# Four of the twelve modulation vectors: their rows weighed and added on GpSimd, the partitions summed on TensorE

## The chip, the cores and the metric

The kernel runs on one core of a Trainium2 chip. The metric is the device time of one execution in microseconds (us), as the median of several runs. The core has TensorE (PE in the profile, with its weight loads as PEld), VectorE (DVE), ScalarE (ACT), GpSimd (POOL) and SyncE (SP, which here issues nearly all DMA transfers). SBUF and PSUM are the on-chip memories; PSUM has eight banks, numbered 0 to 7, into which TensorE writes.

## What is computed

Two layers of a diffusion backbone work on 384 tokens: 128 of a prompt and 256 of a sample, each with 1024 channels. Each layer first turns a condition vector (one for the prompt, one for the sample) into six modulation vectors of 1024 numbers, and uses them around its mixers and its FFN:

```python
mod = (jax.nn.silu(cond) @ lp["w_mod"] + lp["b_mod"])[:, None, :]
sh1, sc1, g1, sh2, sc2, g2 = jnp.split(mod, MOD_CHUNKS, axis=-1)
h = rms_norm(x, lp["norm1"]) * (1 + sc1) + sh1
o, new_ctx = token_mixers(h, lp, ctx_cache, rope_a, rope_b)
x = x + g1 * o
h = rms_norm(x, lp["norm2"]) * (1 + sc2) + sh2
x = x + g2 * conv_ffn(h, lp)
```

`w_mod` of a layer has 1024 rows and 6144 columns in fp32, 24 MB. `token_mixers` projects `h` once and runs grouped-query attention (GQA, branch A, 8 heads of 64), multi-head latent attention (MLA, branch B) and a Hyena long convolution (branch C); three gates and three branch projections are merged and projected out.

The vectors are numbered v = 0 to 5 in the order of the split. So v = 3 and 4 (`sh2`, `sc2`) are first needed when the FFN of their layer begins, and v = 5 (`g2`) where its result is added to x.

## The kernel before

**Main products.** Every large product is made of blocks of 128 channels by 384 tokens. `mm3` (lines 268 to 271) makes one fp32 product from three matmuls over split parts: high by high, high by low, low by high. `load_w` (line 247) brings a block of weights by a DMA from SP (line 249) into one of two 1 MB slots (`raw_ring`, inside the slab `base`), copies its high part with ScalarE (line 231) and subtracts it with VectorE (line 235) into the slab `split`.

**Modulation.** `mod_vec` (line 332) makes one of the twelve vectors: four DMAs of 1 MB through the same `raw_ring`, 16 fp32 matmuls of 512 columns whose stationary operand has 32 columns, the condition vectors (line 338; they run in four groups of four, and the profile has two records for each fp32 matmul, so a group shows as x8), a ScalarE copy of 128x512 out of PSUM, four transposes (line 302) and two additions on VectorE. It uses the PSUM line `md`, which is bank 7 and nobody else's.

**Order within a layer.** `weave` (line 1334) advances a main generator and, at given rates, side generators. Layer 0 goes: first Hyena projections; the others with the Hyena chain (`hyena_chain`) beside them; the attention projections; then gates 2, branch 2, gates 0, branch 0, gates 1 with the attention (`att`: `prep`, then `gqa`, then `mla`) beside them; branch 1; the output projection; the FFN. Branch 0 needs GQA's result `oA`, branch 1 MLA's `oB`. In layer 0 v = 2 to 5 are one side chain (`md`, rate 0.24) beside all that; v = 4 of layer 1 comes after the vectors that were begun in layer 0's FFN. On top of this a tile scheduler, which simulates the program in time while it is built, fixes each engine's final order; at run time each engine works its list strictly in that order.

**Attention.** `attention` (line 906) makes scores (line 922), a softmax (`softmax`, line 885: row maximum on VectorE, lines 891 and 892, exponentials on ScalarE, line 894, the scaling on VectorE), transposes (line 302), ScalarE copies and the product with the values (line 954). Its PSUM tiles come from the line `at`, which has banks 3 to 6.

**Banks.** `ps_of(line, ...)` takes the next bank of a line's list, and `banks(...)` sets the lists for each stage:

```python
PS_HY0 = {"mm": "123", "tr": "46", "fl": "05"}
PS_HY1 = {"mm": "0123", "tr": "4", "ch": "56"}
PS_AT = {"mm": "012", "at": "3456"}
PS_OUT = {"mm": "0123", "tr": "456"}
```

Two tiles in one bank follow each other in program order: the later one's first write waits until the earlier one has been read.

**GpSimd** holds 133 instructions. Most belong to the Hyena chain: 128x256 additions and products (line 709) and 128x128 copies (line 658). Products of 128x768 (line 566) and attention copies (line 875) are among the rest.

## Time and profile before

| | us |
|---|---|
| three runs | 1506.55, 1504.46, 1502.84 |
| median | 1504.46 |
| the profiled execution | 1503.74 |
| its span in the profile | 1501.6 |

The mean granted TensorE clock of the profiled execution is 0.992 of full speed. Of the span, PE is busy for 97%, VectorE 67%, ScalarE 50% and GpSimd 7%; the 16 DMA engines are busy for about 43%. A "wait" row says which engine, tile and line waited, and for what. A group row gives a line, engine, operation, output and input with their shapes, a count, and then its busy time, the mean length of one in ns and the idle time of the engine before it. Matmuls overlap in the records (one of 384 columns shows 0.34 us, while the next begins 0.17 to 0.18 us later), so their price is read from the starts of successive rows.

### The profile page before, as it was taken

The numbers are of one execution on the slowest core, as the hardware profiler recorded it, in microseconds if no ns is written. First come the engines' busy times: TensorE is split into PE (matmuls) and PEld (weight loads), VectorE is DVE, ScalarE is ACT, GpSimd is POOL, SyncE is SP. The second block draws the span as 40 slices with busy tenths as digits, with TensorE's granted clock in tenths as the row PEclk, the third lists the DMA queues.
The fourth block names the chain that finished last, engine by engine and source line by source line (L and its number), as shares of the span: only waits on it lengthen the run. The fifth ranks groups of instructions, "written<-read, shape, count | busy, mean of one in ns | idle before, by whom it ended". The sixth has DMA issues, their size and how long they took to land.

```text
span 1501.6 us, 22071 instructions
## 1 busy us (share of the span) xinstructions
PE 1455.7 (97%) x8542; PEld 1337.6 (89%) x8542; DVE 1006.0 (67%) x1920; ACT 751.3 (50%) x1376; POOL 106.4 (7%) x133
## 2 busy tenths in 40 slices
PE   5799999999999999999998999999999999999997
PEld 2588789989889899999996988999888989999997
DVE  6768569547457896686766767884655767567674
ACT  4545356555544663463545444855555454344343
POOL 1223210000000001010000212100000000000000
PEclk9899999999999999999999999999999999999999
DMA  9444454433466543343276446332333523433431
GB/s 362 151 153 138 136 166 138 119 113 113 141 224 228 187 137 103 122 130 113 85 246 204 139 135 182 91 106 83 97 118 111 195 100 117 135 105 122 153 119 50
DMA packets 177496, 212.84 MB, mean 142 GB/s; under 512 B 24176, under 2 KB 160112, under 8 KB 177392
## 3 DMA queue, kind: packets, MB, share of 16 engines
q1 hardware_dynamic: 176528, 206.99, 42.7%
q0 software_dynamic: 864, 4.46, 1.0%
q8 instruction: 67, 1.10, 0.3%
q14 instruction: 37, 0.30, 0.1%
HBM read 209.29 MB, written 2.13 MB: 141 GB/s over the span
## 4 chain that ended last, share of the span: by engine, by line
PE 90%; DVE 4%; ACT 3%; DMA 2%; issue 1%; SPq 0%; DVEq 0%; ACTq 0%
PE banks L269 26%; PE banks L270 26%; PE banks L271 25%; PE banks L302 3%; PE banks L338 3%; PE banks L922 3%; DVE s L238 2%; PE banks L954 2%; DMA base<-in_w_in_dram 1%; DVE split L235 1%; PE banks L558 1%; ACT split L231 1%; ACT s L231 1%; PE banks L503 0%; DVE s L241 0%
## 5 line engine op out<-in xcount | busy, mean ns | idle before, releaser
L231 ACT ACTIVATE split<-base 128x1024 fp32r<-128x1024 f32 (+2 forms) x272 | 280.9, 1041 | 366.9 <-PE banks L270 258.5
L235 DVE TENSOR_TENSOR split<-base,split 128x1024 fp32r<-128x1024 f32 (+2 forms) x272 | 331.8, 1225 | 181.5 <-ACT split L231 179.4
L269 PE MATMUL banks<-h,split 128*128 128x384 f32 x1280 | 433.3, 342 | 5.0 <-DVE h L403 3.6
L270 PE MATMUL banks<-h,split 128*128 128x384 f32 x1280 | 435.2, 340 | 0.1
L271 PE MATMUL banks<-h,split 128*128 128x384 f32 x1280 | 434.2, 340 | 0.0
L269 PEld LDWEIGHTS banks<-h,split 128*128 128x128 f32 x1280 | 241.4, 189 | 20.7 <-issue 9.9
L270 PEld LDWEIGHTS banks<-h,split 128*128 128x128 f32 x1280 | 242.0, 189 | 4.5 <-issue 1.3
L271 PEld LDWEIGHTS banks<-h,split 128*128 128x128 f32 x1280 | 241.7, 189 | 2.2 <-issue 0.5
L270 PE MATMUL banks<-s,split 128*128 128x384 f32 x672 | 225.8, 337 | 0.0
L271 PE MATMUL banks<-s,split 128*128 128x384 f32 x672 | 225.4, 338 | 0.0
L269 PE MATMUL banks<-s,split 128*128 128x384 f32 x672 | 223.2, 339 | 1.0 <-ACT s L231 0.8
L241 DVE SCALAR_TENSOR_TENSOR s<-banks,base,s 128x127 f32<-128x127 f32 (+1 forms) x448 | 172.8, 411 | 11.9 <-ACT s L417 7.9
L231 ACT ACTIVATE s<-banks 128x384 f32<-128x384 f32 (+11 forms) x212 | 94.3, 471 | 99.1 <-PE banks L271 37.9
L231 ACT ACTIVATE s<-s 128x384 fp32r<-128x384 f32 (+3 forms) x142 | 79.0, 562 | 106.0 <-DVE s L238 57.2
L269 PEld LDWEIGHTS banks<-s,split 128*128 128x128 f32 x672 | 125.6, 188 | 4.4 <-ACT s L231 1.4
L271 PEld LDWEIGHTS banks<-s,split 128*128 128x128 f32 x672 | 126.1, 188 | 2.0 <-DVE base L241 0.8
L270 PEld LDWEIGHTS banks<-s,split 128*128 128x128 f32 x672 | 126.1, 188 | 1.4 <-issue 0.2
L238 DVE TENSOR_TENSOR s<-banks,s 128x512 f32<-128x512 f32 (+3 forms) x132 | 81.6, 645 | 37.7 <-PE banks L271 16.7
L241 DVE SCALAR_TENSOR_TENSOR base<-banks,base 128x128 f32<-128x128 f32 (+1 forms) x128 | 46.9, 413 | 73.8 <-PE banks L271 73.8
L238 DVE TENSOR_TENSOR s<-s 128x256 f32<-128x256 f32 (+4 forms) x122 | 69.0, 576 | 23.0 <-ACT s L1225 8.4
L417 ACT ACTIVATE s<-banks,base 128x384 f32<-128x384 f32 x112 | 73.2, 655 | 13.2 <-PE banks L271 13.2
L302 PE MATMUL banks<-base,s 128*128 128x128 f32 x442 | 75.2, 274 | 2.8 <-DVE s L241 1.7
(146 smaller groups left out, 1730.4 us busy)
## 6 DMA issues: line engine op xcount, KB each, us to landing
base<-in_w_in_dram SPq DMA_DIRECT2D x40, 1024.0 KB, 5.4
base<-in_ffn_up_dram SPq DMA_DIRECT2D x40, 1024.0 KB, 5.1
base<-in_w_mod_dram SPq DMA_DIRECT2D x28, 1024.0 KB, 5.3
s<-in_w_mod_dram SPq DMA_DIRECT2D x14, 1024.0 KB, 7.5
base<-in_ffn_down_dram SPq DMA_DIRECT2D x16, 896.0 KB, 4.6
base<-in_w_branch_dram SPq DMA_DIRECT2D x24, 512.0 KB, 3.5
base<-in_w_out_dram SPq DMA_DIRECT2D x8, 1024.0 KB, 5.1
base<-in_ffn_down_dram SPq DMA_DIRECT2D x8, 1024.0 KB, 5.0
```

The source lines that it names most:

```text
L231: act.activation(out=out, in_=in_, func=AF.Copy, scale=scale)
L235: dve.tensor_tensor(out=lo, in0=src, in1=f(hi), op=ALU.subtract)
L238: dve.tensor_tensor(out=out, in0=a, in1=b, op=op)
L241: dve.scalar_tensor_tensor(out=out, in0=a, scalar=s, in1=b, op0=op0, op1=op1)
L269: pe.matmul(out, l[0], r[0], start=start, stop=False)
L270: pe.matmul(out, l[0], r[1], start=False, stop=False)
L271: pe.matmul(out, l[1], r[0], start=False, stop=stop)
L302: pe.transpose(out, in_, ident[:n, :n])
L338: pe.matmul(gv[32 * j:32 * j + 32], cT[:, 2 * k + j // 2], raw[:, j // 2, (j % 2) * 512:(j % 2) * 512 + 512], start=k == 0, stop=k == KD / ...
L417: act.activation(out=dst, in_=src, func=AF.Identity, scale=vec(l, w1), bias=vec(l, bias))
L922: pe.matmul(out, q_of(h)[:, i * 128:(i + 1) * 128], k, start=m == 0, stop=m == len(ks) - 1)
L954: last = pe.matmul(p[b:b + 64, u], v, pT, start=start, stop=stop, tile_position=(0, b)).ins
```

## The change

Three vectors of layer 0 (v = 3, 4, 5) and one of layer 1 (v = 4) leave `mod_vec` and are made by the new `mod_pool`. It works on half a vector, 512 columns, at a time. For each of the 8 blocks of 128 rows of `w_mod` a DMA of 256 KB brings 128x512 numbers into a ring of two slots in the slab `extra`; GpSimd multiplies them by the condition of the sample and of the prompt (two `tensor_scalar`, one number per partition) and adds them to two accumulators (two `tensor_tensor`, none for the first block). So the 1024 rows become 128 partial rows on the partitions. At the end `sums_of` lets TensorE sum over the partitions: 8 matmuls whose stationary operand is a 128x128 piece of the accumulator and whose moving operand is one column of ones. Their results go to PSUM line `tr`, and VectorE adds the bias. v = 3 and 4 are woven (rate 0.8) beside the Hyena and attention projections and finished in program order before the attention begins; v = 5 beside branch 1 and the output projection.

```diff
+    def mod_pool(l, vs):
+        ring, accs, pr_b = Ring(XO, 2, 512), Ring(XO, 2, 1024), XO.alloc(512)
+        late = []
+        def sums_of(v, hf, acc):
+            pm = ps_of("tr", 4, 2)
+            for q in range(4):
+                for s in range(2):
+                    pe.matmul(
+                        pm[:, q, s:s + 1], acc[:, s, q * 128:(q + 1) * 128], ones[:, 0:1], start=True, stop=True
+                    )
+            o = v * 8 + 4 * hf
+            out = mods[l][:, o:o + 4]
+            tt(out, pm, vecs[l][:, V_B + o:V_B + o + 4].unsqueeze(2).to_broadcast([128, 4, 2]), ALU.add)
...
+        for v, hf in [(v, hf) for v in vs for hf in range(2)]:
+            acc = accs.get().ap(2, 512)
+            col = v * 1024 + hf * 512
+            for k in range(KD):
+                raw = ring.get().ap()
+                sp.dma_start(out=raw, in_=w_mod[l, k * 128:(k + 1) * 128, col:col + 512])
+                parts = [pr_b.ap(), raw] if k else [acc[:, 1], acc[:, 0]]
+                for s, out in zip((1, 0), parts):
+                    pool.tensor_scalar(out=out, in0=raw, scalar1=cT[:, k, s:s + 1], scalar2=None, op0=ALU.mult)
+                    if k:
+                        pool.tensor_tensor(out=acc[:, s], in0=acc[:, s], in1=out, op=ALU.add)
+                yield
+                if k == 3 and late:
+                    sums_of(*late.pop(0))
+                    yield
+            late.append((v, hf, acc))
...
+        sums_of(*late.pop(0))
...
     for l in range(NL):
-        md = chain(*[mod_vec(l, v) for v in (2, 3, 4, 5)]) if l == 0 else chain(nxt.pop().steps, mod_vec(l, 4))
+        md = mod_vec(l, 2) if l == 0 else nxt.pop().steps
+        mp = mod_pool(l, (3, 4) if l == 0 else (4,))
         banks(**PS_HY0)
-        weave(main, (md, R_MD), (fl, R_FL))
+        weave(main, (md, R_MD), (mp, R_MP), (fl, R_FL))
...
-        weave(attn_proj(l, hT, proj), (md, R_MD), (ch, R_CH))
+        weave(attn_proj(l, hT, proj), (md, R_MD), (mp, R_MP), (ch, R_CH))
+        finish(mp)
         finish(ch)
         hyena_close(y)
         banks(**PS_AT)
...
-        weave(branch(l, 1, gs, oB, m, merged), (md, R_MD))
+        mp = mod_pool(l, (5,)) if l == 0 else iter(())
+        weave(branch(l, 1, gs, oB, m, merged), (md, R_MD), (mp, R_MP))
...
-        weave(out_proj(l, merged), (ah.loads, R_AH))
+        weave(out_proj(l, merged), (ah.loads, R_AH), (mp, R_MP))
+        finish(mp)
```

In counts: 128 records of modulation matmuls, 16 transposes, 4 ScalarE copies of 128x512 and 16 DMAs of 1 MB go; 64 one-column matmuls, 128 GpSimd multiplications and 112 GpSimd additions of 128x512 and 64 DMAs of 256 KB come. GpSimd's list grows from 133 to some 373 instructions. The lines after the new function move: mm3's three matmuls are now 271 to 273, transposes 304, the scores 968, the product with the values 1000, the Hyena chain's operations 704 and 755; the new DMA is line 390, the multiplication 393, the addition 395, the sums 374.

**TensorE, layer 0, beside the GQA.** The order before, with L269 to L271 the main products (here of branch 2), L922 the scores and L302 the transposes:

```order
L338 MATMUL banks<-base_101 32x512 x4
L269 MATMUL banks<-s_2_702,split_362 128x384
L270 MATMUL banks<-s_2_702,split_362 128x384
L271 MATMUL banks<-s_2_702,split_362 128x384
L302 MATMUL banks<-base_101,s_1_141 128x128 x8
L269 MATMUL banks<-s_2_702,split_362 128x384
L270 MATMUL banks<-s_2_702,split_362 128x384
L271 MATMUL banks<-s_2_702,split_362 128x384
L922 MATMUL banks<-s_4_1554,s_1_135 128x384
L922 MATMUL banks<-s_2_734,s_1_135 128x384
```

The main products stood between the steps of the attention. The order after, at the fourth group of sums (L374), with L271 to L273 the last main products of gates 0, L304 the transposes and L968 the scores:

```order
L271 MATMUL banks<-h_363,split_362 128x384
L272 MATMUL banks<-h_363,split_362 128x384
L273 MATMUL banks<-h_363,split_362 128x384
L374 MATMUL banks<-base_101,extra_470 128x1 x8
L304 MATMUL banks<-base_101,s_1_110 128x128 x4
L968 MATMUL banks<-s_4_1725,s_1_135 128x128
L968 MATMUL banks<-s_2_781,s_1_135 128x128
```

All main products up to the end of gates 0 now stand ahead of the sums, and the attention's first scores behind them. Some 30 rows later on TensorE, in the middle of the same GQA:

```order
L304 MATMUL banks<-base_101,s_1_110 128x128 x6
L968 MATMUL banks<-s_4_1725,s_1_135 128x384
L968 MATMUL banks<-s_2_781,s_1_135 128x384
L304 MATMUL banks<-base_101,s_1_138 128x128 x6
L968 MATMUL banks<-s_4_1725,s_1_135 128x384
L968 MATMUL banks<-s_2_781,s_1_135 128x384
L304 MATMUL banks<-base_101,s_1_141 128x128 x12
```

No main product stands between the attention's steps there any more.

**GpSimd, layer 0, the Hyena chain.** Before:

```order
L658 COPY s_1_107<-s_1_107 128x128 x3
L709 TENSOR_TENSOR s_1_141<-s_1_141,s_1_138 128x256 x2
L709 TENSOR_TENSOR s_1_138<-s_1_138,s_1_141 128x256 x2
L658 COPY s_1_107<-s_1_107 128x128 x2
L709 TENSOR_TENSOR s_1_138<-s_1_138 128x256 x2
```

After:

```order
L395 TENSOR_TENSOR extra_470<-extra_470 128x512
L755 TENSOR_TENSOR s_1_141<-s_1_141,s_1_138 128x256 x2
L704 COPY s_1_107<-s_1_107 128x128
L393 TENSOR_SCALAR extra_470<-extra_470,base_101 128x512
L755 TENSOR_TENSOR s_1_138<-s_1_138,s_1_141 128x256 x2
L395 TENSOR_TENSOR extra_470<-extra_470 128x512
L393 TENSOR_SCALAR extra_470<-extra_470,base_101 128x512
L704 COPY s_1_107<-s_1_107 128x128
```

The chain's instructions (now L704 and L755) have the new multiplications and additions between them.

**SP, layer 0, around the attention projections.** Before, with L249 the weights of `load_w` and L329 the 1 MB loads of `mod_vec`:

```order
L329 DMA base_101<-in_w_mod_dram 128x2x1024
L249 DMA base_101<-in_w_in_dram 128x8x256
L1111 DMA base_101<-in_mla_w_ukv_dram 128x4x64 x4
L249 DMA base_101<-in_w_branch_dram 128x4x256 x4
L249 DMA base_101<-in_w_in_dram 128x8x256 x2
L329 DMA base_101<-in_w_mod_dram 128x2x1024
```

After, with the last four loads of layer 0's v = 4 (L390; L251 is `load_w`):

```order
L390 DMA extra_470<-in_w_mod_dram 128x512
L251 DMA base_101<-in_w_branch_dram 128x4x256
L390 DMA extra_470<-in_w_mod_dram 128x512
L251 DMA base_101<-in_w_branch_dram 128x4x256
L390 DMA extra_470<-in_w_mod_dram 128x512
L251 DMA base_101<-in_w_in_dram 128x8x256
L390 DMA extra_470<-in_w_mod_dram 128x512
```

The small loads of the modulation weights stand one by one between the loads of branch and gate weights.

## Rows read from the trace of the kernel before

**Rows 1.** Page: busy time by engine, then the chain that ended last

```profile
PE 1455.7 (97%) x8542; PEld 1337.6 (89%) x8542; DVE 1006.0 (67%) x1920; ACT 751.3 (50%) x1376; POOL 106.4 (7%) x133
...
PE 90%; DVE 4%; ACT 3%; DMA 2%; issue 1%; SPq 0%; DVEq 0%; ACTq 0%
```

**Rows 2.** PE's waits: line, releaser: us in total, times, longest us

```profile
PE banks L464 <- ACT s L436: 8.6, 1, 8.6
...
PE banks L269 <- DVE h L403: 3.6, 2, 2.3
...
PE banks L269 <- ACT split L231: 0.8, 2, 0.5
```

**Rows 3.** Windows: us, busy of PE, PEld, DVE, ACT, POOL, PEclk, DMA share, GB/s

```profile
245.90:341.30 95.40, 93.75 (x599) 85.52 (x599) 54.88 (x103) 53.41 (x120) 0.45 (x3) 1.00 0.44 125
130.00:216.00 86.00, 86.00 (x476) 71.91 (x475) 55.96 (x95) 37.34 (x68) 21.28 (x22) 1.00 0.48 157
480.00:520.00 40.00, 39.40 (x241) 30.98 (x240) 31.57 (x72) 25.28 (x43) 1.27 (x2) 1.00 0.60 196
520.00:580.00 60.00, 60.00 (x353) 59.26 (x353) 49.72 (x100) 34.33 (x56) 2.56 (x3) 1.00 0.32 106
```

**Rows 4.** Timeline of PE: start us, length, around one group of mod_vec

```profile
237.58 0.34 PE L271 MATMUL banks<-h,split 128*128 128x384 f32 x1
237.85 1.06 PE L338 MATMUL banks<-base 128*32 128x512 f32 x8
...
239.13 0.34 PE L270 MATMUL banks<-h,split 128*128 128x384 f32 x1
```

**Rows 5.** The same, around four transposes

```profile
235.16 0.34 PE L270 MATMUL banks<-h,split 128*128 128x384 f32 x1
235.34 0.60 PE L302 MATMUL banks<-base,s 128*128 128x128 f32 x4
...
235.95 0.34 PE L269 MATMUL banks<-h,split 128*128 128x384 f32 x1
```

**Rows 6.** The same, around four fp32 matmuls of one column (x8 records)

```profile
727.78 0.33 PE L271 MATMUL banks<-h,split 128*128 128x384 f32 x1
727.95 0.95 PE L538 MATMUL banks<-base,s 128*128 128x1 f32 x8
...
729.02 0.33 PE L270 MATMUL banks<-h,split 128*128 128x384 f32 x1
```

**Rows 7.** The same, around two scores of layer 0's GQA

```profile
249.79 0.51 PE L922 MATMUL banks<-s,s 128*128 128x384 f32 x2
250.14 0.33 PE L269 MATMUL banks<-s,split 128*128 128x384 f32 x1
```

**Rows 8.** ScalarE's groups from 245.9 to 341.3 us: busy, mean ns, idle before

```profile
L894 ACT ACTIVATE s<-banks,s 128x384 f32<-128x384 f32 x16 | 9.1, 575 | 12.2 <-DVE s L892 12.1
L231 ACT ACTIVATE extra<-banks 128x384 f32<-128x384 f32 x12 | 5.7, 495 | 5.5 <-PE banks L302 5.4
L894 ACT ACTIVATION_READ_ACCUMULATOR s<-banks,s 128x1 f32 x24 | 4.9, 205 | 0.0
...
L231 ACT ACTIVATE s<-banks 128x512 f32<-128x512 f32 x8 | 4.6, 589 | 0.9 <-PE banks L302 0.9
...
L894 ACT ACTIVATE s<-banks,s 128x128 f32<-128x128 f32 x8 | 2.8, 385 | 0.0
```

**Rows 9.** GpSimd by line: shortest, median, longest ns, first and last start

```profile
L709 POOL TENSOR_TENSOR s<-s,s x28: 730/830/1717, 114.4 to 936.4; 128x256 f32<-128x256 f32 x28
...
L566 POOL TENSOR_TENSOR s<-s,s x8: 1812/1843/2755, 39.7 to 753.0; 128x768 f32<-128x768 f32 x8
...
L875 POOL COPY s<-s x6: 397/430/1408, 221.0 to 979.7; 128x256 f32<-128x256 f32 x6
```

**Rows 10.** GpSimd's group of the Hyena chain, whole span: busy, mean ns, idle

```profile
L709 POOL TENSOR_TENSOR s<-s,s 128x256 f32<-128x256 f32 x28 | 28.7, 1044 | 51.4 <-DVE s L238 36.9 <-DVE base L238 14.3
```

**Rows 11.** VectorE's low parts of the weights: shortest, median, longest ns

```profile
L235 DVE TENSOR_TENSOR split<-base,split x272: 1082/1224/2293, 48.4 to 1477.7; 128x1024 fp32r<-128x1024 f32 x112, 128x896 fp32r<-128x896 f32 x20, 128x960 fp32r<-128x960 f32 x4
```

More of the change, by code (lines that the diff above doesn't have):

```diff
@@ L45 @@
 R_F0 = 3
+R_MP = 0.8
 U_CH, U_MLA = 20, 20
@@ L203 @@
     FA = Arena([Slab(ctx, tc, n, f"s{i}") for i, n in enumerate(SLABS)])
-    XA = Arena([Slab(ctx, tc, N_EXTRA, "extra"), *FA.slabs])
+    extra = Slab(ctx, tc, N_EXTRA, "extra")
+    XO, XA = Arena([extra]), Arena([extra, *FA.slabs])
     RA = Rounded(FA)
@@ L360, in mod_vec @@
         yield
+    def mod_pool(l, vs):
[11 more added lines that the diff above has]
+            tt(out, pm, vecs[l][:, V_B + o:V_B + o + 4].unsqueeze(2).to_broadcast([128, 4, 2]), ALU.add)
+            if v in (1, 4):
+                n = (V_N1, V_N2)[v // 4] + 4 * hf
+                g = vecs[l][:, n:n + 4].unsqueeze(2).to_broadcast([128, 4, 2])
+                stt(avs[l][:, v // 4, 4 * hf:4 * hf + 4], out, 1.0, g, ALU.add, ALU.mult)
+        for v, hf in [(v, hf) for v in vs for hf in range(2)]:
[14 more added lines that the diff above has]
+            late.append((v, hf, acc))
+        for _ in range(4):
+            yield
+        sums_of(*late.pop(0))
+        ring.free()
+        accs.free()
+        pr_b.free()
     def rstd_of(out, squares):
@@ L1407 @@
         ch = urgent(chain(hyena_chain(y, 0), hyena_chain(y, 1)), U_CH)
-        weave(hyena_in(y, 1, hT), (md, R_MD), (ch, R_CH))
+        weave(hyena_in(y, 1, hT), (md, R_MD), (mp, R_MP), (ch, R_CH))
         while y.late:
```

## Prediction

> **What bounds the kernel now.** I read the shares by engine and the chain that ended last, then PE's waits, then windows of the stages that the change touches. PE is busy for 97% of the span and carries 90% of the chain [rows 1]. Its longest waits (8.6 us and 3.6 us) stand at single places, and in the whole span it waited at the main products for the split weights' high parts for 0.8 us [rows 2]. From 245.9 to 341.3 us, where layer 0's GQA runs, PE is busy for 93.75 of 95.4 us, although ScalarE and VectorE work on the softmax at the same time (53.4 and 54.9 us) [rows 3]. So there are two ways to move the time: take work from PE, which counts in full, or take away what keeps PE busy while it waits for others. The change does the first on purpose and, by the order, the second as well. A change of less than 0.3%, 4.5 us, can't be told from none here. I work from the profiled execution, 1503.74 us, which lies 0.7 us below the median.
>
> **Work taken from PE.** A group of four modulation matmuls delays the stream by 239.13 - 237.58 = 1.55 us, less two main matmuls of 0.175, so 1.20 us [rows 4]. A vector has four groups: 4.80. Its four transposes cost 235.95 - 235.16 - 0.35 = 0.44 [rows 5]. So 5.24 us for a vector, and for four vectors 21.0 us go.
>
> **Work given to PE.** The sums are fp32 matmuls with a full stationary operand and one column. The rows have them at line 538: four of them delay the stream by 729.02 - 727.78 - 0.35 = 0.89 us [rows 6]. A vector has 16, so 3.56; four vectors 14.2 us. Net, PE wins 21.0 - 14.2 = 6.8 us: what is left of a matmul when its columns are taken away is nearly all its weight load. With nothing else the time would be 1503.7 - 6.8 = 1496.9. The four ScalarE copies and the larger DMAs that go lay beside PE and give nothing.
>
> **The GQA loses its cover.** This is the largest term, and it comes from one bank. From `PS_HY1` on, line `tr` has only bank 4; the sums of v = 3 and 4 go there, and the attention's line `at` begins with banks 3 to 6. Since `finish(mp)` stands before the attention in the program, a score in bank 4 has to stand behind the last sums, and the scheduler put these behind GpSimd's work as it simulated it: the fourth group of sums stands behind the last block of gates 0 in TensorE's order. Before, the GQA ran between the products of the gates and of branch 2. Now these have all been done, the next ones (branch 0) need the GQA's own result, and from the fourth sums to the GQA's end the order has 30 wide scores, 16 scores of 128 columns, some 72 transposes, 32 products with the values and 12 main matmuls.
>
> PE's own work there: wide scores 0.35 / 2 = 0.175 each [rows 7], 30 x 0.175 = 5.3; transposes 0.44 / 4 = 0.11, the narrow scores taken the same, 88 x 0.11 = 9.7; values about 0.12, between the two, 3.8; 12 x 0.175 = 2.1; the sums 1.8. Together 22.7 us.
>
> ScalarE's work for the same: 16 exponentials of 384 with their reads of the sum, 16 x (0.575 + 0.205) = 12.5; 8 of 128, 8 x (0.385 + 0.205) = 4.7; 16 copies of 128x384 at 0.495, 7.9; 9 copies of 128x512 at 0.589, 5.3 [rows 8]. That is 30.4 us. With the 12.1 us for which it waited, before those 16 exponentials, for the row maximum that VectorE had just scaled [rows 8], 42.5. The softmaxes overlap (three are in flight), so part of these waits goes, but each has to go from PE to VectorE, ScalarE, VectorE and back. I take 40 us, near the upper of the two, since that row shows the wait in this same code. The stall is then 40 - 23 = 17 us. Lower bound: ScalarE never waits, 30.4 - 22.7 = 8. Upper: 42.5 and another 5.4 us for waiting at the transposes, as in the row of the copies to `extra` [rows 8]: 47.9 - 22.7 = 25.
>
> Nothing gives this back later: the products that covered the GQA were done ahead of it, where PE was busy anyway, so the stall is added to the end. What is late next is branch 0, which waits for `oA`.
>
> **The wait at the fourth sums.** GpSimd's additions of 512 columns aren't in the trace; between 0.73 for 256 (the shortest of line 709) and 1.81 for 768 (the shortest of line 566) lies 1.27 us. A multiplication reads one tensor: the 256-column copy's 0.40 us, scaled like the addition, gives 0.69 [rows 9]. A step of two and two takes 3.9 us undisturbed, and 32 steps 125 us; doubled by the chain and by waits, 250 us from a start near 45, so it is done before the 310 us or so at which the fourth sums stand. But the last four loads stand singly between weight loads on SP, and their slots come free only as GpSimd goes on. I bound the wait by 0 and one step with its loads, 5 us, and take 2.
>
> **The Hyena chain.** From 130 to 216 us GpSimd was busy for 21.3 of 86 us [rows 3]; in the order 23 multiplications and 20 additions now stand between the chain's own instructions, 23 x 0.69 + 20 x 1.27 = 41 us, so some 62 of 86. Each of the 48 operations of line 709 in both layers (28 of the form in [rows 10], 20 of another) can find one foreign addition ahead of it: 48 x 1.27 = 61 us of delay. GpSimd stood idle for 51.4 us before 28 of them, waiting for VectorE [rows 10], and PE hardly ever waits for the chain, so most of it is slack. I take a twentieth, 3 us; the bounds are 0 and an eighth, 8.
>
> **VectorE.** Its subtraction of the low parts, with two inputs from SBUF, takes 1.22 us at the median and 2.29 at the longest, and GpSimd's line 709 goes from 0.83 to 1.72 [rows 9, 11]: the two engines disturb each other at times. Where GpSimd is now busy all through, VectorE has 30 us idle of 86 in the chain's window and 10.3 of 60 in the tightest one [rows 3]. I take 1 us, bounds 0 and 3.
>
> **Sum.** 1503.7 - 6.8 + 17 + 2 + 3 + 1 = 1519.9, so **1520 us**, 1.0% slower. By the terms' lower ends 1503.7 - 6.8 + 8 = 1505, by the upper ones 1496.9 + 25 + 5 + 8 + 3 = 1538.
>
> **Rival B, the GQA stays fed (faster).** If the stalls before the scores are filled, that is, if the elapsed time of the block is PE's own 23 us, and the GpSimd work is slack throughout, only the 6.8 us are left: 1497. For it speaks that before the change PE had 93.75 of 95.4 us busy with the same softmaxes; against it that then some 300 main matmuls stood in the stretch, and now 12. It decides where ScalarE's 30 us and its waits fit under PE's: with 30.4 against 22.7 they don't. Chance 0.08. Between B and the forecast lies the case that ScalarE hardly waits and the small terms come to nothing, 1505, inside the 0.3%: 0.08.
>
> **Rival C, VectorE is locked out by GpSimd.** In the stretch from 480 to 580 us v = 5 brings 32 multiplications and 28 additions, 32 x 0.69 + 28 x 1.27 = 58 us. VectorE has 8.4 + 10.3 = 18.7 us idle there [rows 3]. If GpSimd keeps it from working for two thirds of its own time, 39 us, then 20 us come on top of the forecast: 1540. A third is absorbed, and that is the point from which it decides. The medians close to the shortest (0.83 to 0.73 and 1.22 to 1.08) speak against it, the longest for it, at single instructions [rows 9, 11]. Chance 0.06.
> The Trainium skill, page "SBUF — State Buffer", section on the two separate sides of SBUF, says that a VectorE instruction with two SBUF inputs and a GpSimd instruction that reads SBUF take one shared pair of ports as a lock for a whole instruction, so that the other blocks fully. The longest cases (2.29 against 1.22, 1.72 against 0.83) agree with one such block; by that rule whole GpSimd instructions would be lost to VectorE, and the rival's 1540 is the result.
>
> **Rival D, it does not do what it says.** Should the sums of v = 3 and 4 wait for GpSimd much longer than one step (its price nearer 1.8 than 1.27 for an addition and as much for a multiplication: 32 x 7.2 = 230 us, and more with the chain between), PE would stand still at the fourth sums with nothing behind them that can pass: 20 us more is 1540 too. Its chance is 0.04.
>
> **Chances.** Forecast 0.74, between 1509 and 1533; B 0.08; the small stall 0.08; C 0.06; D 0.04. Faster by over 0.3% 0.08, within 0.3% 0.08, slower 0.84. The range is **1504 to 1538**: it leaves out B and the greater part of C and D.
>
> **What will show it.** In the profile after: right behind the fourth group of sums (L374, about 310 us) a stretch of some 40 us in which PE is busy for little over half, with waits at the scores and transposes for VectorE and ScalarE; elsewhere no new waits of size. The 16 groups of sums should delay the stream by 0.89 us each, GpSimd's additions should take 1.3 to 1.6 us and its multiplications about 0.7, and the one wait at L374 should be under 5 us. I am wrong if PE is as busy beside the GQA as before (then B), if the additional waits lie between 480 and 580 us at the split weights (C), or if one long wait stands at L374 (D).

## The result

The changed kernel takes 1559.7 us (median; 1558.1 to 1561.6) against 1503.9 us before (1502.8 to 1506.6): the ratio is 1.0369, with a 95% interval of 1.0354 to 1.0385. It is 55.8 us slower. Slower was forecast, but by 16 us, and the range ended at 1538.

The page of the changed kernel, in the parts that answer to [rows 1]: busy time by engine, PE and granted clock in 40 slices, and the chain that ended last.

```profile
span 1557.3 us, 22365 instructions
PE 1471.9 (95%) x8526; PEld 1362.2 (87%) x8526; DVE 1080.5 (69%) x1922; ACT 749.1 (48%) x1372; POOL 516.9 (33%) x373
...
PE   6799998969999999999999899999999999999997
...
PEclk9799998969999999999999999999999999999999
...
PE 80%; DVE 8%; POOL 4%; DMA 3%; ACT 3%; issue 2%; SPq 0%; DVEq 0%; ACTq 0%; POOLq 0%
```

PE's share of the chain fell from 90% to 80%; VectorE's doubled to 8%, and GpSimd came in with 4%. GpSimd's busy time rose by 410 us, and VectorE's by 74 us although it has only two instructions more.

**Where they are lost.** The two profiled executions differ by 55.7 us. The main products are the same 6288 matmuls in both kernels, in the same order, so the start of the n-th one is a clock to compare by. I gave each PE instruction the usual distance to its successor for its form, from the trace of before, and called the rest stall. Each cell is after less before, in us:

| main matmuls | reached before, after | PE's own work | stall |
|---|---|---|---|
| to 96 (start, filters) | 89.6, 99.0 | -0.1 | +9.6 |
| 96 to 768 (projections, Hyena chain) | 265.4, 277.6 | -8.5 | +11.2 |
| 768 to 1056 (gates, GQA, up to branch 0) | 358.5, 405.6 | +4.8 | +30.1 |
| 1056 to 1536 (gates 1, MLA, branch 1) | 478.6, 523.1 | -2.9 | +0.3 |
| 1536 to 2016 (FFN's beginning) | 581.0, 641.4 | +1.8 | +14.1 |
| the rest, with layer 1 | 1491.8, 1547.4 | -1.6 | -3.1 |
| sum | | -6.5 | +62.2 |

So TensorE gained what was worked out for it, and lost 62 us, nearly all in four places. Not all of the stall is waiting. By the two pages PE's idle time rose by 39.5 us (45.9 before, 85.4 after); the other 22.7 us are its own instructions taking longer than usual, with a mean granted clock of 0.973 against 0.992. The table rests on one profiled execution of each kernel, and the runs of one kernel below differ by up to 5.6 us, so 2 or 3 us in a cell decide nothing.

**GpSimd's prices**, to set beside [rows 9]: shortest, median, longest ns, then first and last start; and the same two groups on the page, with busy time and mean ns.

```profile
L393 POOL TENSOR_SCALAR extra<-extra,base x128: 1552/1664/3607, 45.4 to 684.9; 128x512 f32<-128x512 f32 x128
...
L395 POOL TENSOR_TENSOR extra<-extra x112: 1255/1296/2324, 51.0 to 687.5; 128x512 f32<-128x512 f32 x112
```

```profile
L393 POOL TENSOR_SCALAR extra<-extra,base 128x512 f32<-128x512 f32 x128 | 244.6, 1916 | 123.9 <-PE banks L1000 66.7
...
L395 POOL TENSOR_TENSOR extra<-extra 128x512 f32<-128x512 f32 x112 | 165.2, 1486 | 1.4
```

The addition's shortest is 1.26 us, as interpolated. The multiplication, with one tensor to read, takes 1.55 us at its shortest and 1.92 us on average.

**The GQA.** PE's timeline from the last main matmul of gates 0 to the first scores (start us, length, idle before in brackets), then windows with the columns of [rows 3]:

```profile
315.66 0.34 PE L273 MATMUL banks<-h,split 128*128 128x384 f32 x1
323.80 3.58 PE L374 MATMUL banks<-base,extra 128*128 128x1 f32 x16 [7.80 <-POOL extra L395]
327.63 1.12 PE L304 MATMUL banks<-base,s 128*128 128x128 f32 x4 [0.26 <-DVE base L240]
330.15 1.11 PE L968 MATMUL banks<-s,s 128*128 128x128 f32 x4 [1.40 <-DVE s L240]
```

```profile
300.00:320.00 20.00, 15.99 (x93) 15.67 (x91) 6.21 (x4) 6.13 (x9) 16.59 (x11) 1.00 0.33 103
320.00:340.00 20.00, 11.38 (x45) 9.71 (x46) 5.84 (x12) 5.55 (x21) 3.66 (x3) 0.50 0.14 44
340.00:360.00 20.00, 16.77 (x103) 12.60 (x104) 14.80 (x26) 12.89 (x38) 0.00 (x0) 0.82 0.03 7
...
323.80:375.00 51.20, 40.95 (x230) 31.56 (x230) 28.62 (x52) 27.73 (x82) 0.45 (x3) 0.77 0.01 3
```

The reader is to see four things. PE stands for 7.8 us at the fourth sums, waiting for GpSimd's last addition. Behind the wait the granted clock is 0.50, that is 1.2 GHz: these sums take 3.58 us, while the second group, at 2.4 GHz, took 1.84 us (its row is below). And from 320 to 340 us PE has 45 instructions where a stretch of main products has over a hundred. Over the whole bare GQA (the last row) PE is nevertheless busy for 41 of 51 us, at a mean granted clock of 0.77: it idles for 10 us, and the rest of what is lost is its own work taking longer. The last product of the GQA with the values starts at 371 us; so the bare GQA took some 44 us from the sums.

```profile
197.04 1.84 PE L374 MATMUL banks<-base,extra 128*128 128x1 f32 x16
```

**VectorE.** The same line in the window from 40 to 110 us, before and then after (busy, mean ns, idle before):

```profile
L235 DVE TENSOR_TENSOR split<-base,split 128x1024 fp32r<-128x1024 f32 x10 | 14.1, 1411 | 9.6 <-ACT split L231 9.6
L238 DVE TENSOR_TENSOR s<-banks,s 128x512 f32<-128x512 f32 x15 | 10.0, 684 | 4.7 <-PE banks L558 3.3 <-ACT s L231 1.4
```

```profile
L237 DVE TENSOR_TENSOR split<-base,split 128x1024 fp32r<-128x1024 f32 x8 | 14.9, 1866 | 12.4 <-ACT split L233 12.4
L240 DVE TENSOR_TENSOR s<-banks,s 128x512 f32<-128x512 f32 x17 | 11.1, 681 | 0.4 <-ACT s L233 0.4
```

The subtraction, whose inputs both come from SBUF, went from 1.41 to 1.87 us; the addition that reads PSUM stayed at 0.68. Over the whole span, 244 two-input VectorE instructions without PSUM overlap a GpSimd instruction; they take 302 ns more on average than the quick ones of their form, 74 us together (before: 77 of them, 17 us). The 104 that read PSUM and overlap lose 3 ns. The 28 tensor_scalar and 6 casts within SBUF that overlap lose some 350 ns each as well.

**The FFN's beginning.** The window from 500 to 640 us with the columns of [rows 3], before and then after:

```profile
500.00:640.00 140.00, 139.41 (x813) 136.84 (x812) 102.96 (x199) 71.11 (x106) 7.50 (x7) 1.00 0.37 118
```

```profile
500.00:640.00 140.00, 129.69 (x752) 117.83 (x751) 122.07 (x198) 69.26 (x111) 114.80 (x68) 0.98 0.52 169
```

GpSimd is busy for 115 us of it instead of 7.5, and VectorE for 122 instead of 103. This is not the work for v = 5 alone. GpSimd works from 440 to 689 us without a longer pause on two vectors, v = 5 and layer 1's v = 4: the latter needs only the condition and its weights, nothing ties it to layer 1, and it was taken forward into layer 0 (in the kernel with layer 1's v = 4 alone it runs from 390 to 508 us).

### The profile page after: what moved, and what is told of

Same layout as the page of the kernel before. It is cut to its first block, busy times and chain, and to the rows that moved or that the text cites. A ratio compares the mean times of both kernels' runs of the same rounds, so it can differ in the third digit from the quotient of the medians.

```text
span 1557.3 us, 22365 instructions
## 1 busy us (share of the span) xinstructions
PE 1471.9 (95%) x8526; PEld 1362.2 (87%) x8526; DVE 1080.5 (69%) x1922; ACT 749.1 (48%) x1372; POOL 516.9 (33%) x373
## 4 chain that ended last, share of the span: by engine, by line
PE 80%; DVE 8%; POOL 4%; DMA 3%; ACT 3%; issue 2%; SPq 0%; DVEq 0%; ACTq 0%; POOLq 0%
PE banks L271 23%; PE banks L272 23%; PE banks L273 23%; PE banks L304 3%; DVE s L240 3%; PE banks L968 2%; POOL extra L393 2%; DVE split L237 2%; PE banks L1000 1%; DMA extra<-in_w_mod_dram 1%; PE banks L340 1%; POOL extra L395 1%; DVE s L243 1%; DMA base<-in_w_in_dram 1%; PE banks L374 1%
## 5 line engine op out<-in xcount | busy, mean ns | idle before, releaser
L237 DVE TENSOR_TENSOR split<-base,split 128x1024 fp32r<-128x1024 f32 (+2 forms) x272 | 353.7, 1303 | 168.3 <-ACT split L233 167.5
L271 PE MATMUL banks<-h,split 128*128 128x384 f32 x1280 | 431.8, 341 | 7.8 <-DVE h L449 3.6
L273 PE MATMUL banks<-h,split 128*128 128x384 f32 x1280 | 433.7, 339 | 0.0
L393 POOL TENSOR_SCALAR extra<-extra,base 128x512 f32<-128x512 f32 x128 | 244.6, 1916 | 123.9 <-PE banks L1000 66.7
L271 PEld LDWEIGHTS banks<-h,split 128*128 128x128 f32 x1280 | 241.7, 189 | 18.1 <-DVE h L449 5.9
L273 PEld LDWEIGHTS banks<-h,split 128*128 128x128 f32 x1280 | 241.7, 189 | 2.2 <-issue 0.7
L271 PE MATMUL banks<-s,split 128*128 128x384 f32 x672 | 226.7, 344 | 6.1 <-DVE s L243 4.0
L273 PE MATMUL banks<-s,split 128*128 128x384 f32 x672 | 226.1, 339 | 0.0
L395 POOL TENSOR_TENSOR extra<-extra 128x512 f32<-128x512 f32 x112 | 165.2, 1486 | 1.4
L233 ACT ACTIVATE s<-banks 128x384 f32<-128x384 f32 (+10 forms) x212 | 94.3, 472 | 122.5 <-PE banks L304 56.1
L271 PEld LDWEIGHTS banks<-s,split 128*128 128x128 f32 x672 | 126.8, 190 | 9.8 <-DVE s L243 4.3
L273 PEld LDWEIGHTS banks<-s,split 128*128 128x128 f32 x672 | 127.2, 190 | 1.6 <-DVE base L243 0.8
L240 DVE TENSOR_TENSOR s<-banks,s 128x512 f32<-128x512 f32 (+3 forms) x132 | 81.7, 644 | 31.5 <-PE banks L273 12.1
L240 DVE TENSOR_TENSOR s<-s 128x256 f32<-128x256 f32 (+4 forms) x122 | 81.2, 677 | 30.1 <-ACT s L567 11.4
```

Source lines behind the costliest of these rows:

```text
L233: act.activation(out=out, in_=in_, func=AF.Copy, scale=scale)
L237: dve.tensor_tensor(out=lo, in0=src, in1=f(hi), op=ALU.subtract)
L240: dve.tensor_tensor(out=out, in0=a, in1=b, op=op)
L271: pe.matmul(out, l[0], r[0], start=start, stop=False)
L273: pe.matmul(out, l[1], r[0], start=False, stop=stop)
L393: pool.tensor_scalar(out=out, in0=raw, scalar1=cT[:, k, s:s + 1], scalar2=None, op0=ALU.mult)
```

## The experiments

The first table gives the measured time of each kernel beside the kernel before on the same chip, and the added stall of its profiled execution by the stretches above. Of the two stretches left out, 1056 to 1536 has 10.8 us in e18, 6.1 in e14 and between -3 and 0.3 in the others, the rest between -6 and 2.

| kernel | us (before) | to 96 | 96 to 768 | 768 to 1056 | 1536 to 2016 |
|---|---|---|---|---|---|
| changed kernel | 1559.7 (1503.9) | 9.6 | 11.2 | 30.1 | 14.1 |
| e1: sums in bank 7 | 1529.1 (1505.4) | 9.6 | 8.9 | 10.9 | 12.2 |
| e8: v = 4 back | 1513.8 (1505.4) | 8.3 | 0.8 | -0.1 | 12.4 |
| e15: e8, and bank 4 held | 1544.7 (1503.9) | 9.1 | 6.9 | 19.3 | 12.4 |
| e13: slab held, no sums | 1545.0 (1504.8) | 8.9 | 9.9 | 23.9 | 0.1 |
| e11: half the GpSimd work | 1514.1 (1504.8) | 6.5 | -1.6 | -0.1 | 12.1 |
| e2: v = 5 back | 1536.6 (1505.4) | 8.6 | 7.6 | 21.7 | 3.3 |
| e9: GpSimd work, unused | 1516.1 (1505.4) | 7.6 | 1.1 | 3.5 | 6.0 |
| e14: e9 with memsets | 1522.8 (1504.5) | 5.8 | -3.5 | 4.9 | 6.8 |
| e10: v = 3 and layer 1 | 1515.9 (1504.8) | 10.3 | -1.8 | 7.6 | 6.5 |
| e12: e10, begun late | 1519.4 (1504.5) | 2.3 | 8.4 | 13.2 | 2.5 |
| e18: other multiplication | 1582.1 (1503.9) | 13.4 | 25.1 | 3.3 | 34.2 |
| e3: layer 1 alone | 1503.5 (1504.8) | 0.3 | -0.1 | 0.0 | 2.9 |

### What holds the GQA

**The sums of v = 3 and 4 in bank 7** (after v = 2, its only other user, is finished):

```diff
+            if l == 0 and v != 5:
+                finish(md)
-            pm = ps_of("tr", 4, 2)
+            pm = ps_of("md" if l == 0 and v != 5 else "tr", 4, 2)
```

> The changed kernel, but the sums of layer 0's v = 3 and 4 go to bank 7, which no attention tile uses, instead of bank 4. In the order the scores and transposes of the GQA stand among the main products again; its last products with the values still stand bare. Theory A (a hold through bank 4 takes the cover from the GQA and is most of the loss, some 40 us between the last main products before the fourth sums and branch 0): about 30 us of it go, 1530 us (1520 to 1540). Rival B (GpSimd's work slows VectorE and its lateness does the harm everywhere; the GQA is only where it shows): 1550 us or more.

1529.1 us, a ratio of 1.0168 (1.0151 to 1.0184): theory A's number. One bank's name is worth 30 us. Some 11 us of stall stay beside the GQA (the stretch is 16 us longer than before).

**v = 4 of layer 0 back on TensorE**, so that the last sums ahead of the attention are done at 195 us:

```diff
-        md = mod_vec(l, 2) if l == 0 else nxt.pop().steps
-        mp = mod_pool(l, (3, 4) if l == 0 else (4,))
+        md = chain(mod_vec(l, 2), mod_vec(l, 4)) if l == 0 else nxt.pop().steps
+        mp = mod_pool(l, (3,) if l == 0 else (4,))
```

> The changed kernel, but v = 4 of layer 0 is made by TensorE as before; v = 3 and 5 and layer 1's v = 4 stay on GpSimd. Layer 0's last sums ahead of the attention are then done long before it, so neither bank 4 nor the memory of the slab holds the GQA. TensorE gets 1.7 us more work. Theory A: the 40 us beside the GQA go, the losses at the start (10 us) and in the FFN's beginning (14 us) stay: 1521 us (1514 to 1529). Rival B: the shorter GpSimd work takes a third of the loss, 1541 us.

1513.8 us (ratio 1.0063, 1.0046 to 1.0080), just under the range of theory A: the whole stall beside the GQA is gone, and that of the stretch ahead of it too, which I had not expected to go with it.

**Bank 4 alone.** The same kernel, in which GpSimd goes on after v = 3 on 512 columns of zeros, and an unused group of sums goes to bank 4:

```diff
+        if l == 0 and vs[0] == 3:
+            held = XO.alloc(512)
+            w = held.ap()
+            pool.memset(w, 0.0)
+            for k in range(16):
+                for s in range(2):
+                    pool.tensor_scalar(out=w, in0=w, scalar1=cT[:, k % 8, s:s + 1], scalar2=None, op0=ALU.mult)
+                    if k % 8:
+                        pool.tensor_tensor(out=w, in0=w, in1=w, op=ALU.add)
+                yield
+            pm = ps_of("tr", 4, 2)
...
+                    pe.matmul(pm[:, q, s:s + 1], w[:, q * 128:(q + 1) * 128], ones[:, 0:1], start=True, stop=True)
```

> The kernel with v = 4 of layer 0 back on TensorE and v = 3, 5 and layer 1's v = 4 on GpSimd, with one thing more: after v = 3 GpSimd works on for as many multiplications and additions as v = 4 had, on zeros in 512 columns, without loads, and a group of eight one-column matmuls of it goes to bank 4; nothing uses it. The slab keeps room for the GQA's transposed weights, so this holds bank 4 alone. TensorE's order beside the GQA is then as in the changed kernel. Theory A (bank 4 alone is enough to take the GQA's cover): 1514 + 30 = 1544 us (1534 to 1553). Rival (the slab was the hold, the order alone costs little): 1516 to 1522 us.

1544.7 us, as theory A had it. No copy into the slab waits for GpSimd here. This run parts the order from the wait; PE's timeline at those sums (line 420) and windows of it:

```profile
314.09 0.33 PE L273 MATMUL banks<-h,split 128*128 128x384 f32 x1
314.26 1.84 PE L420 MATMUL banks<-base,extra 128*128 128x1 f32 x16
316.43 0.66 PE L304 MATMUL banks<-base,s 128*128 128x128 f32 x4 [0.33 <-DVE extra L421]
318.49 1.11 PE L984 MATMUL banks<-s,s 128*128 128x128 f32 x8 [1.40 <-DVE s L240]
```

```profile
300.00:320.00 20.00, 18.03 (x113) 17.57 (x112) 7.26 (x7) 5.21 (x9) 13.13 (x9) 0.99 0.33 106
320.00:340.00 20.00, 14.71 (x60) 11.41 (x60) 13.74 (x24) 12.29 (x42) 0.00 (x0) 0.58 0.00 0
```

Here PE doesn't wait for GpSimd at all, the sums follow the last main matmul at once; yet the stall from 768 to 1056 is 19.3 us, where the kernel without the tie has none. It is the order that costs: the main products have gone ahead, and the GQA stands alone. VectorE's two-input instructions lose under 3 us in this stretch, so it is not GpSimd's disturbance. The granted clock falls here too, to 0.58 on average from 320 to 340 us, behind waits of a microsecond or so. From the sums to the end of the last product with the values, 314.3 to 359.5 us, PE is busy for 35.5 of 45.2 us and idles for 9.7: about half of the 19.3 us is waiting, the other half its own work taking longer, most of it before 340 us. How much would be left at the full clock no run shows.

**The slab alone.** All vectors as before, with GpSimd's work for v = 3 and 4 unused beside them, and without sums:

```diff
-        md = mod_vec(l, 2) if l == 0 else nxt.pop().steps
-        mp = mod_pool(l, (3, 4) if l == 0 else (4,))
+        md = chain(*[mod_vec(l, v) for v in (2, 3, 4, 5)]) if l == 0 else chain(nxt.pop().steps, mod_vec(l, 4))
+        mp = mod_pool(l, (3, 4)) if l == 0 else iter(())
...
+            if l == 0:
+                return
             pm = ps_of("tr", 4, 2)
...
-        mp = mod_pool(l, (5,)) if l == 0 else iter(())
+        mp = iter(())
```

> The kernel before with all vectors made as before, and GpSimd's new work and DMAs for v = 3 and 4 of layer 0 beside it, without the sums; the results are not used. Nothing of it is in bank 4, but the ring and the accumulators take the slab in which the GQA's transposed weights are put, until GpSimd is done. Theory A (the slab is a second hold, and explains the 17 us that stayed beside the GQA when the sums went to bank 7): start 9 and GQA 15, 1528 us (1520 to 1536). Rival (the slab costs nothing, the rest in that kernel was the wait for the sums in TensorE's order): start 9 alone, 1511 to 1515 us.

1545.0 us, dearer than theory A's 1528. There is a second hold, and it is in these rows: the copy of the GQA's transposed weights into `extra` waits for GpSimd's last addition (line 397), and PE's scores for that copy.

```profile
ACT extra L233 <- POOL extra L397: 7.3, 1, 7.3
```

```profile
PE banks L970 <- ACT extra L233: 8.0, 1, 8.0
```

Bank and slab don't add up (19 and 24 us alone, 30 together): either leads to the same order. Here too no main product stands on PE between 320.8 and 354 us.

**Half of GpSimd's work** for v = 3 and 4 (the sample's share is left out, and the prompt's accumulator is summed twice):

```diff
-                for s, out in zip((1, 0), parts):
+                for s, out in (zip((0,), parts[1:]) if l == 0 and v != 5 else zip((1, 0), parts)):
...
-                        pm[:, q, s:s + 1], acc[:, s, q * 128:(q + 1) * 128], ones[:, 0:1], start=True, stop=True
+                        pm[:, q, s:s + 1], acc[:, 0 if l == 0 and v != 5 else s, q * 128:(q + 1) * 128], ones[:, 0:1], start=True, stop=True
```

> The changed kernel with half of GpSimd's work for v = 3 and 4 of layer 0: only the prompt's multiplication and addition are made, and its accumulator is summed for both streams; the DMAs, sums, banks and the slab stay. In the order the fourth sums then stand earlier and the GQA among the main products. Theory A (the hold lasts as long as GpSimd works, and its multiplication, 1.9 us and not 0.7, is what made it long): beside the GQA 30 of 40 us go, at the start some 4: 1526 us (1518 to 1535). Rival (bank 4 costs the same however early GpSimd is done): 1550 us or more.

1514.1 us, under the expected range: with bank and slab as they were, the stall beside the GQA is gone. TensorE's order changed with the edit: GpSimd is done at 213 us, the main products stand among the GQA's steps again, and PE waits at no sums. So the holds cost only where GpSimd's work reaches the attention; the losses at the start (6.5 us) and at the FFN (12 us) stay.

### What is lost elsewhere

**v = 5 back on TensorE:**

```diff
-        md = mod_vec(l, 2) if l == 0 else nxt.pop().steps
+        md = chain(mod_vec(l, 2), mod_vec(l, 5)) if l == 0 else nxt.pop().steps
...
-        mp = mod_pool(l, (5,)) if l == 0 else iter(())
+        mp = iter(())
```

> The changed kernel, but v = 5 of layer 0 is made by TensorE, in one chain with v = 2. GpSimd has no new work between 400 and 850 us. Theory A (v = 5 on GpSimd costs some 14 us around the FFN's beginning, because VectorE is slowed there where it is tight): 1559.7 - 14 + 1.7 = 1547 us (1543 to 1551). Rival (the loss lies beside the GQA alone, and what shows between 520 and 640 us only follows from it): 1559 to 1562.

1536.6 us, under the range of theory A. The stall at the FFN's beginning falls from 14.1 to 3.3 us (10.8 and not 14). The expectation had a wrong premise, that GpSimd has no new work after 400 us: layer 1's v = 4 runs there, from 431 to 555 us. Another 8 us are saved beside the GQA, since in this kernel the fourth sums wait for 0.8 us and not 7.8. Why GpSimd ends its work there 6 us earlier was not settled.

**GpSimd's work alone**, for v = 3 and 5, unused, without sums; all vectors on TensorE (the edit is that of the slab's kernel with `(3,)` for `(3, 4)` and v = 5 kept on GpSimd too):

> The kernel before with all twelve vectors made as before, and GpSimd's new work for v = 3 and v = 5 of layer 0 beside it, DMAs, multiplications and additions in the places where the change puts them, without the sums on TensorE; the results are not used. So it adds nothing to TensorE and shows what GpSimd's work alone does to the others. Theory A (it slows VectorE and the Hyena filters at the start by 10 us, the FFN's beginning by 12 to 14): 1504 + 23 = 1527 us (1518 to 1533). Rival (GpSimd's work is hidden, the losses there come from where sums and loads were put): 1504 to 1509.

1516.1 us (ratio 1.0075, 1.0059 to 1.0091), between the two: 7.6 us at the start and 6 at the FFN. It is not hidden. At the FFN more than half of the changed kernel's 14 us is missing, and so is layer 1's v = 4. Over all kernels with these instructions but the one with the other multiplication, this stall goes with GpSimd's busy time in the stretch from 1536 to 2016: some 100 us of it go with 12 to 14 us (the changed kernel, e1, e8, e11, e15), 29 to 43 us with 2.5 to 6.5 (e2, e3, e9, e10, e12), and 2.6 us with 0.1 (e13).

**Begun late.** First v = 3 and layer 1's v = 4 alone, with `mod_pool` left out of the first weave, then with a tie to the last filter:

```diff
-        weave(main, (md, R_MD), (mp, R_MP), (fl, R_FL))
+        weave(main, (md, R_MD), (mp if l else iter(()), R_MP), (fl, R_FL))
```

> v = 3 of layer 0 and v = 4 of layer 1 on GpSimd, the others on TensorE; v = 3 begins only after the first Hyena projections and filters. So GpSimd has no new work in the start (9 us lost there in all kernels that have it) and none at the FFN. TensorE's own work falls by 3.4 us. Theory A (the loss is three places: start, GQA, FFN's beginning): all three go, 1504 - 3.4 + some 3 for the Hyena chain = 1504 us (1499 to 1509). Rival (each GpSimd instruction costs VectorE time wherever it stands): 1512 or more.

```diff
+        if l == 0 and vs[0] == 3:
+            for b in ring.bufs:
+                copy_a(b.ap()[:, 0:1], f(y.spec[1][1].ap()[:, 0, 0:1]))
```

> As the kernel with v = 3 of layer 0 and v = 4 of layer 1 on GpSimd, but a ScalarE copy of one column ties the ring of v = 3 to the last filter, so that GpSimd's new work really begins after the Hyena filters of layer 0 (in the other kernels the scheduler took it from 45 us on). Theory A (the loss of 9 to 10 us before the first 96 main matmuls is GpSimd's work beside the filters): that loss is gone, at most 2 us left there. The work then ends later and holds the slab longer, which may cost up to 10 us beside the GQA: 1508 us (1503 to 1516). Rival (the start loses its time through the loads of 256 KB or the place of the sums): 8 us or more stay before the first 96 main matmuls.

The first missed: 1515.9 us, in the rival's range, but it tests neither, with 10.3 us lost at the start as ever. Its GpSimd work begins at 47.6 us all the same; the scheduler had taken the instructions forward, since nothing tied them. With the tie the first multiplication starts at 108.5 us, and the loss at the start falls to 2.3 us: so it is the work beside the filters. But the time is 1519.4 us. GpSimd's work moved under the Hyena chain and nearer to the GQA, where 8.4 and 13.2 us are lost instead; the loss moves with the work.

**Lock or queue.** Does GpSimd's reading keep VectorE from working (a lock), or do GpSimd's own instructions for filters and Hyena chain stand behind the new ones (its queue)? The kernel with unused work, each GpSimd operation replaced by a memset, which reads nothing:

```diff
-                for s, out in zip((1, 0), parts):
-                    pool.tensor_scalar(out=out, in0=raw, scalar1=cT[:, k, s:s + 1], scalar2=None, op0=ALU.mult)
-                    if k:
-                        pool.tensor_tensor(out=acc[:, s], in0=acc[:, s], in1=out, op=ALU.add)
+                pool.memset(whole, 0.0)
+                pool.memset(whole, 0.0)
+                if k:
+                    pool.memset(whole[:, 0:1472], 0.0)
+                    pool.memset(whole[:, 0:1472], 0.0)
```

> As the kernel with the extra, unused GpSimd work for v = 3 and 5, but each multiplication and addition is replaced by a memset of about the same length (1792 and 1472 columns), behind the same DMAs and in nearly the same places of GpSimd's order. GpSimd is as busy and as late for the filters and the Hyena chain, but reads nothing from SBUF. Theory L (GpSimd's reading instructions and VectorE's with two SBUF inputs exclude each other): VectorE's subtraction of the low parts goes back to 1.23 us on average, less than half of the 8 us at the start stays, 1509 us (1505 to 1512). Rival Q (the loss is GpSimd's queue: its own filter and chain instructions stand behind the new ones): as with the real work, 8 us at the start and 1516 us (1513 to 1520).

1522.8 us: neither theory's total. By place it splits. In the Hyena chain's stretch the stall is gone (theory L), and over the span VectorE's two-input instructions without PSUM lose 16 us instead of 42, no more than in the kernel before (17). From 40 to 110 us the subtraction takes 1.40 us on average, as before. At the start 5.8 of 7.6 us stay, as rival Q wants; but there VectorE's tensor_scalar and casts now lose some 5 us, so the queue isn't shown by it. And a new loss appears that nobody expected, at a VectorE tensor_scalar with one input; VectorE's timeline, then GpSimd's:

```profile
432.41 6.49 DVE L946 TENSOR_SCALAR s<-s 128x384 f32<-128x384 f32 x1
438.82 1.21 DVE L237 TENSOR_TENSOR split<-base,split 128x1024 fp32r<-128x1024 f32 x1
```

```profile
431.74 1.60 POOL L393 MEMSET extra<- 128x1792 f32 x1
433.28 1.33 POOL L396 MEMSET extra<- 128x1472 f32 x1
434.55 1.60 POOL L394 MEMSET extra<- 128x1792 f32 x1
436.09 1.33 POOL L397 MEMSET extra<- 128x1472 f32 x1
437.35 1.33 POOL L396 MEMSET extra<- 128x1472 f32 x1
438.74 1.42 POOL L397 MEMSET extra<- 128x1472 f32 x1
```

That instruction takes 0.42 us elsewhere. Here it lasts until a memset ends at 438.7 us: it stood through five memsets in a row. That they shut it out is read from the two timelines. A second one, at 502.6 us, lasted 4.40 us, and PE waited 4.9 us behind it; so most of the 6.8 us at the FFN is not the loss of the real work there (6.0 us), and this run can't tell what that was.

**Another form of the multiplication**, as tensor_tensor with the condition repeated along the row:

```diff
-                    pool.tensor_scalar(out=out, in0=raw, scalar1=cT[:, k, s:s + 1], scalar2=None, op0=ALU.mult)
+                    pool.tensor_tensor(out=out, in0=raw, in1=cT[:, k, s:s + 1].to_broadcast([128, 512]), op=ALU.mult)
```

> The changed kernel with each of GpSimd's multiplications written as a tensor_tensor of the block with the condition's column, repeated along the row, instead of a tensor_scalar. Bank, slab, loads and sums stay. In the order made with it the GQA stands among the main products, since the scheduler takes GpSimd to be done earlier. Theory A (the multiplication's length decides how long bank and slab are held; the new form takes 1.3 us like the additions): the loss beside the GQA falls by 25 to 30 us, 1528 us (1515 to 1537). Rival (the new form takes as long as the old, so TensorE, in its new order, waits for the sums instead): 1545 us or more.

1582.1 us, the slowest of all, and in the rival's range. The multiplication did get shorter (median 1.15 us instead of 1.66, GpSimd busy for 442 us instead of 517), and beside the GQA only 3.3 us are lost, as theory A said. The rival's reason holds in part: TensorE, in its new order, waits 11.6 us for GpSimd's additions at three groups of sums.

```profile
PE banks L374 <- POOL extra L395: 11.6, 3, 5.5
```

And VectorE is slowed more than ever: its subtractions from 40 to 110 us take 2.21 us, against 1.87 and 1.41, and 181 two-input instructions lose 564 ns each, 102 us together.

```profile
L237 DVE TENSOR_TENSOR split<-base,split 128x1024 fp32r<-128x1024 f32 x8 | 17.6, 2214 | 6.7 <-ACT split L233 6.7
```

The order changed with the form, and GpSimd's work stands denser (v = 3 and 4 are done at 265 us and not at 324). So the run doesn't part the form from the order, nor the waits for GpSimd from VectorE's loss.

**Layer 1 alone:** the kernel before with v = 4 of layer 1 on GpSimd, `mod_pool` called for nothing else:

> The kernel before with a single vector moved to GpSimd, v = 4 of layer 1; layer 0 is as before. TensorE's own work falls by 1.7 us; in the changed kernel the same stretch of layer 1 got some 5 us back. Theory A (the sums are a gain where nothing waits for them and GpSimd is not in a tight stretch): 1500 us (1497 to 1503). Rival (GpSimd's work slows VectorE and the Hyena chain in layer 1 as it does in layer 0, and eats the 1.7 us): 1507 or more.

1503.5 us beside 1504.8, a ratio of 0.9989 (0.9980 to 0.9998). It is faster than the kernel before by 1.4 us, near the 1.7 us of TensorE's work, and not by the 5 us that I expected. It is within what I called no change. GpSimd's work is not in layer 1, as I had thought, but beside the end of layer 0, and costs 2.9 us at the FFN's beginning.

## Why the prediction was wrong

**TensorE's own work was right.** -6.8 us forecast, -6.5 by the counts and usual distances of the table. A group of 16 records delays the stream by 1.79 us, read as in [rows 6], twice 0.89.

**Beside the GQA the order was right, and the size partly luck.** That the bank puts the main products ahead and leaves the GQA bare was read from the order, and 17 us of stall were put on it; the kernel with bank 4 held and no wait measured 19.3. But the 17 us were to be waits for the softmax, with PE busy for little over half of some 40 us. The waits came to 9.7 us, and PE was busy for 35.5 of 45.2 us, where its own work had been put at 22.7. Left out was what the idle time does next: the granted clock was 0.58 from 320 to 340 us there, and 0.50 in the changed kernel. The two errors nearly cancel.

**The first step that failed is GpSimd's multiplication.** It was scaled from the copy of one input, 0.69 us, because it reads one tensor; it takes 1.55 at the shortest and 1.92 on average. So a step of two and two takes 5.6 us undisturbed and 6.8 in the run, not 3.9. GpSimd was to be done after 250 us, at some 295, and ended v = 4 at 324; the wait at the fourth sums was 7.8 us against 2, above its upper end of 5. That the wait was not longer is luck: 32 steps of 6.8 are 218 us and took 278, so the doubling of the forecast for chain and waits was too much and hid most of the wrong price. Rival D had nearly this price, 7.2 us a step, and a chance of 0.04, but put 20 us more on the wait.

**The second is VectorE, 1 us with bounds 0 and 3.** It is the term that missed by most: at the FFN alone 14.1 us were lost, where VectorE was busy for 122 of 140 us and most of PE's waits were for it. Rival C had the mechanism and the place at the FFN, and 20 us for it; but it stood beside the forecast as a rival, with a chance of 0.06, when it is a term of the same sum. It counted the work for v = 5 alone; with layer 1's v = 4 behind it there were two vectors. The trace of before held the sign: 77 two-input instructions had lost 17 us with GpSimd busy for 106 us [rows 1]. Read as a rate, 517 us of GpSimd would have given some 80 us of VectorE's time, and 74 was measured. I took the medians of [rows 9, 11], which had not moved, and judged the longest to be single cases.
The Trainium skill's page "SBUF — State Buffer", section on the two separate sides, has the rule: a VectorE instruction with two SBUF inputs and a GpSimd instruction that reads SBUF exclude each other, one in a 2-port mode and any GpSimd instruction do too, and one with at most one SBUF input outside those modes is free. Our numbers agree in the first and the last point: 302 ns lost against 3 ns with PSUM, and 16 us instead of 42 once GpSimd reads nothing. Whether the tensor_scalar beside the memsets was in such a mode no run shows; it lasted through five of them, not one.

**The third is the Hyena chain, 3 us with bounds 0 and 8.** From 96 to 768 it was 11.2 us. Nearly all of that went with v = 4 (0.8 us are left with v = 3 alone), so it is the second half of the work, nearer to the attention. PE's one long wait there, 4.0 us at 263 us, was for VectorE, and the granted clock was 0.56 from 260 to 275 us. The memsets cost nothing there, which speaks for VectorE being shut out and not for the queue; they stood for v = 3 alone, so for the 11.2 us it is not shown.

**The fourth is a second hold that I didn't see.** The slab `extra` holds GpSimd's ring and accumulators, and the GQA's transposed weights go there next. The diff shows it, and I spoke only of the bank. It may be why 11 us stayed when the bank was changed: there the copy into the slab waited 3.5 us for GpSimd's last addition. In the changed kernel no such wait stands in the trace, and how much each hold has in it can't be told, since they don't add up.

**The start was not priced at all**, apart from VectorE's 1 us. 9.6 us were lost there. Filters and the first projections share VectorE and GpSimd; the late start moved the loss from 10.3 to 2.3 us. How it divides between the lock and GpSimd's queue is open: with memsets 5.8 of 7.6 us stayed, but VectorE lost time beside these too.

Summed, the forecast's 17 + 2 + 3 + 1 = 23 us of stall are 30 + 11 + 10 + 14 - 3 = 62 in the run. By size, 13 us were missed at the FFN (VectorE's term), 11 beside the GQA with its sums, 9.6 at the start and 8 in the Hyena chain.

## What to carry to other kernels

When work goes to an idle engine, its busy time is not free for an engine that it disturbs: here the time that VectorE's two-input instructions lost was 0.14 to 0.23 us for each microsecond of GpSimd (74 of 517, 102 of 442), and the place where VectorE is tight decides what that is worth. Before a slow engine's result is put into a shared bank or slab, look up who writes there next: the instruction that waits is not the cost, but all that the order puts behind and ahead of it. Look up in the order where the scheduler really puts the new work: what nothing ties is taken forward, as layer 1's v = 4 was. Price an instruction that the trace doesn't show by both kinds of neighbour, and treat a rival whose mechanism is already visible in the rows as a term of the sum.

## What was unexpected of the hardware

On GpSimd a tensor_scalar of 128x512 with a number per partition (1.55 us at the shortest) is slower than a tensor_tensor of two tensors (1.26), and the same product with the number repeated along the row takes 1.03. The kernel with that fastest form cost VectorE more and not less (102 us against 74), though its order differed too. Beside five memsets, which read nothing, one VectorE tensor_scalar lasted 6.49 us, fifteen times its usual length.
